# Advancing the next head pair's prologue beside the current pair's heads in an RWKV-7 layer

## Chip, cores, metric

One Trainium2 chip (trn2), all 8 NeuronCores, no exchange between them: each core runs the whole network on its own eight 256-token segments (or one 2048-token sequence). The metric is the device time of the slowest core in microseconds (us).

## The reference, cut to what matters

Four layers; layers 0 and 2 mix tokens with HGRN2, layers 1 and 3 with RWKV-7, each followed by an MLP. Only RWKV-7 is touched. Per direction, head and token:

```python
r, k, v = rkv[0], rkv[1], rkv[2]                    # three projections of the shifted input
decay = exp(-0.606531 * sigmoid(w0 + tanh(xs1 @ w_la) @ w_lb))
a  = sigmoid(a0 + (xs4 @ a_la) @ a_lb)
kk = k * k_k;  kk = kk / max(sqrt(sum(kk * kk, -1)), 1e-12)      # per head
k  = k * (1 + (a - 1) * k_a)
bonus = sum(r * k * r_k, -1) * v
# scan over tokens (forward, and backward on the flipped sequence)
sa = einsum('bzhvk,bzhk->bzhv', s, kk_t)
s  = s * w_t - sa (x) (kk_t * a_t) + v_t (x) k_t
y_t = einsum('bzhvk,bzhk->bzhv', s, r_t)
```

## The kernel before

A core handles 16 tiles of 128 tokens, per layer and direction. Heads are 64 wide, so 128 channels hold a pair; a tile has 8 pairs (`c`). The kernel records operations in program order (`S.op(engine, ...)`) and derives the semaphore waits from the buffers each reads and writes; every engine has its own list, in the order recorded. All instructions carry the recording helper's line, L200, so a reader goes by tile names.

In names of the profile, PE is TensorE's matmul and PEld its weight load, DVE is VectorE, ACT is ScalarE, POOL is GpSimd, `ps` and `PS[n]` are the program's banks of PSUM, which PE's rows write (`ps<-` in every row shown), and a table load (ACT_TABLE_LOAD, 1283 ns each, 1985 of them in the trace before) is the instruction that stands on ACT three times in each prologue: before the sigmoids, before the square root and before the exponentials.

For each pair there is a prologue, then two head generators advanced in turn, one step (up to a `yield`) per round:

```python
for c in range(8):
    pp = PS[0]
    # 8 + 8 projection matmuls (r, k), 2 low-rank matmuls        PE  -> pp
    # sg, aa = sigmoid(...)                                      ACT (table load)
    # kk = pk * k_k                                              DVE
    # kk2 = kk * kk                                              POOL
    # block sum of kk2 (matmul with blockones) -> PS[1]          PE
    # rs = max(.), sqrt(rs)                                      DVE, ACT (table load)
    # rs = 1/rs; kk *= rs; t, k2 (into t)                        DVE
    # bb = kk * aa (into aa)                                     POOL
    # prod = r * r_k * k2 (into kk2); head sum -> PS[7]          DVE, PE
    # Ls = scan(sg); Dsg = difference                            DVE
    # wc, emD, eD, emD2 = exp(...); Ds2                          ACT (table load), POOL
    # KB = (k2*eD, bb*eD), QR = (kk*emD2, r*emD)                 POOL, DVE
    # 3 transposes -> PS[1]; KoT, BoTn                           PE, DVE
    def head_gen(c=c, hh=None, ptb=ptb): ...
    run_interleaved([head_gen(hh=0), head_gen(hh=1)], 2)
```

A head generator has 24 steps: 0 opening matmuls of KB and QR (64 rows high); 1 three masked copies on DVE; 2 and 3 right side RH; 4 to 15 six levels of a triangular solve, each a round of fp32 128x128 matmuls and a round of one DVE addition and up to two ACT copies; 16 and 17 matmuls and copies for the chunk maps; 18 to 21 two state updates (DVE scales, PE multiplies, DVE copies back); 22 output matmuls; 23 copy out. I call 18 to 23 the tail, and a pair's join the time from the last head matmul of one pair to the first of the next.

Of the kernel before, what the change touches and what calls it, by code (L numbers as in the profile page):

```python
# [298 lines left out]
def build_program(n_layers=4, mix=True, dbg=False, stop=None):  # L299
# [46 lines left out]
    with contextlib.ExitStack() as st:  # L346
# [548 lines left out]
        def rwkv_layer(l, j, hT, BhT):  # L895
            with contextlib.ExitStack() as ph:
# [51 lines left out]
                ct["prod"] = ct["kk2"]  # L948
# [5 lines left out]
                ct["wc"] = sb(ph, "c_wc", [128, 2])  # L954
# [6 lines left out]
                Bct["prod"] = Bct["kk2"]  # L961
# [12 lines left out]
                for d in range(2):  # L974
# [14 lines left out]
                    for bi, i in enumerate(order):  # L989
# [40 lines left out]
                        for c in range(8):  # L1030
                            cs = slice(c * 128, (c + 1) * 128)
                            S.skip = (_LIM["rstep"] < 4) or (_rt[0] > _LIM["rtiles"])
                            pp = PS[0]
                            for k in range(8):
                                S.op("pe", lambda e, k=k, cs=cs: e.matmul(out=pp[:, 0:128], lhsT=W3[0][:, k, cs], rhs=xsn[0][:, k, :], start=(k == 0), stop=(k == 7)),
                                     reads=[BW3[0], Bxs[0]], writes=[BPS[0]])
                            for k in range(8):
                                S.op("pe", lambda e, k=k, cs=cs: e.matmul(out=pp[:, 128:256], lhsT=W3[1][:, k, cs], rhs=xsn[2][:, k, :], start=(k == 0), stop=(k == 7)),
                                     reads=[BW3[1], Bxs[2]], writes=[BPS[0]])
                            S.op("pe", lambda e, cs=cs: e.matmul(out=pp[:, 256:384], lhsT=wlb[:, cs], rhs=tw[:], start=True, stop=True), reads=[Blo, Btw], writes=[BPS[0]])  # L1040
                            S.op("pe", lambda e, cs=cs: e.matmul(out=pp[:, 384:512], lhsT=alb[:, cs], rhs=ta[:], start=True, stop=True), reads=[Blo, Bta], writes=[BPS[0]])
                            pr, pk = pp[:, 0:128], pp[:, 128:256]
                            S.skip = (_LIM["rstep"] < 5) or (_rt[0] > _LIM["rtiles"])
                            S.op("act", lambda e, c=c: e.activation(out=ct["sg"][:], in_=pp[:, 256:384], func=AF.Sigmoid, bias=vcol(0)[:, c:c + 1], scale=1.0),
                                 reads=[BPS[0], Bvec], writes=[Bct["sg"]])
                            S.op("act", lambda e, c=c: e.activation(out=ct["aa"][:], in_=pp[:, 384:512], func=AF.Sigmoid, bias=vcol(1)[:, c:c + 1], scale=1.0),
                                 reads=[BPS[0], Bvec], writes=[Bct["aa"]])
                            S.op("dve", lambda e, c=c: e.tensor_scalar(out=ct["kk"][:], in0=pk, scalar1=vcol(2)[:, c:c + 1], scalar2=None, op0=ALU.mult),
                                 reads=[BPS[0], Bvec], writes=[Bct["kk"]])
                            S.op("pool", lambda e: e.tensor_tensor(out=ct["kk2"][:], in0=ct["kk"][:], in1=ct["kk"][:], op=ALU.mult), reads=[Bct["kk"]], writes=[Bct["kk2"]])  # L1050
                            S.op("pe", lambda e: e.matmul(out=PS[1][:, 0:128], lhsT=cF["blockones"][:], rhs=ct["kk2"][:], start=True, stop=True),
                                 reads=[Bk, Bct["kk2"]], writes=[BPS[1]])
                            S.op("dve", lambda e: e.tensor_scalar_max(out=ct["rs"][:], in0=PS[1][:, 0:128], scalar1=1e-24), reads=[BPS[1]], writes=[Bct["rs"]])
                            S.op("act", lambda e: e.activation(out=ct["rs"][:], in_=ct["rs"][:], func=AF.Sqrt), reads=[Bct["rs"]], writes=[Bct["rs"]])
                            S.op("dve", lambda e: e.reciprocal(out=ct["rs"][:], in_=ct["rs"][:]), reads=[Bct["rs"]], writes=[Bct["rs"]])
                            S.op("dve", lambda e: e.tensor_tensor(out=ct["kk"][:], in0=ct["kk"][:], in1=ct["rs"][:], op=ALU.mult), reads=[Bct["kk"], Bct["rs"]], writes=[Bct["kk"]])
                            S.skip = (_LIM["rstep"] < 6) or (_rt[0] > _LIM["rtiles"])
                            S.op("dve", lambda e, c=c: e.tensor_scalar(out=ct["t"][:], in0=ct["aa"][:], scalar1=1.0, scalar2=vcol(3)[:, c:c + 1], op0=ALU.subtract, op1=ALU.mult),
                                 reads=[Bct["aa"], Bvec], writes=[Bct["t"]])
                            S.op("dve", lambda e: e.scalar_tensor_tensor(out=ct["k2"][:], in0=ct["t"][:], scalar=1.0, in1=pk, op0=ALU.add, op1=ALU.mult),  # L1060
                                 reads=[Bct["t"], BPS[0]], writes=[Bct["k2"]])
                            S.op("pool", lambda e: e.tensor_tensor(out=ct["bb"][:], in0=ct["kk"][:], in1=ct["aa"][:], op=ALU.mult), reads=[Bct["kk"], Bct["aa"]], writes=[Bct["bb"]])
                            S.op("dve", lambda e, c=c: e.scalar_tensor_tensor(out=ct["prod"][:], in0=pr, scalar=vcol(4)[:, c:c + 1], in1=ct["k2"][:], op0=ALU.mult, op1=ALU.mult),
                                 reads=[BPS[0], Bvec, Bct["k2"]], writes=[Bct["prod"]])
                            S.op("pe", lambda e, c=c: e.matmul(out=PS[7][:, 2 * c:2 * c + 2], lhsT=ct["prod"][:], rhs=cF["headind"][:], start=True, stop=True),
                                 reads=[Bct["prod"], Bk], writes=[BPS[7]])
                            S.skip = (_LIM["rstep"] < 7) or (_rt[0] > _LIM["rtiles"])
# [10 lines left out]
                            S.op("act", lambda e, Lv=Lv: e.activation(out=ct["wc"][:].unsqueeze(2), in_=Lv[:, :, 63:64], func=AF.Exp, scale=-C0), reads=[Bct["Ls"]], writes=[Bct["wc"]])  # L1078
                            S.op("pool", lambda e: e.tensor_tensor(out=ct["Ds2"][:], in0=ct["Dsg"][:], in1=ct["sg"][:], op=ALU.add), reads=[Bct["Dsg"], Bct["sg"]], writes=[Bct["Ds2"]])
                            S.op("act", lambda e: e.activation(out=ct["emD"][:], in_=ct["Dsg"][:], func=AF.Exp, scale=C0), reads=[Bct["Dsg"]], writes=[Bct["emD"]])  # L1080
                            S.op("act", lambda e: e.activation(out=ct["eD"][:], in_=ct["Dsg"][:], func=AF.Exp, scale=-C0), reads=[Bct["Dsg"]], writes=[Bct["eD"]])
                            S.op("act", lambda e: e.activation(out=ct["emD2"][:], in_=ct["Ds2"][:], func=AF.Exp, scale=C0), reads=[Bct["Ds2"]], writes=[Bct["emD2"]])
                            S.skip = (_LIM["rstep"] < 8) or (_rt[0] > _LIM["rtiles"])
# [4 lines left out]
                            S.skip = (_LIM["rstep"] < 9) or (_rt[0] > _LIM["rtiles"])  # L1088
# [9 lines left out]
                            def head_gen(c=c, hh=None, ptb=ptb):  # L1098
                                head = 2 * c + hh
                                prs = slice(64 * hh, 64 * hh + 64)  # L1100
                                hc = slice(head * 64, head * 64 + 64)
                                hcl = slice(hh * 64, hh * 64 + 64)
                                hx = HX[hh]
                                A1, A2, Nmt, Zmt, RH, RpE, P2T, T0p, wch = hx["A1"], hx["A2"], hx["Nm"], hx["Zm"], hx["RH"], hx["RpE"], hx["P2T"], hx["T0p"], hx["wch"]
                                Bh = hx["B"]
                                PA, PB, BA, BB = PS[2 + 2 * hh], PS[3 + 2 * hh], BPS[2 + 2 * hh], BPS[3 + 2 * hh]
                                qr2 = QR[prs, :, :].rearrange("p a t -> p (a t)")
                                S.op("pe", lambda e: e.matmul(out=PA[:, 0:256], lhsT=KB[prs, 0, :], rhs=qr2, start=True, stop=True), reads=[Bct["KB"], Bct["QR"]], writes=[BA])
                                S.op("pe", lambda e: e.matmul(out=PA[:, 256:512], lhsT=KB[prs, 1, :], rhs=qr2, start=True, stop=True), reads=[Bct["KB"], Bct["QR"]], writes=[BA])
                                S.op("pe", lambda e: e.matmul(out=PB[:, 0:128], lhsT=QR[prs, 0, :], rhs=KB[prs, 1, :], start=True, stop=True), reads=[Bct["KB"], Bct["QR"]], writes=[BB])  # L1110
                                yield
                                S.op("dve", lambda e: e.tensor_tensor(out=A1[:], in0=PA[:, 0:256], in1=mk1[:], op=ALU.mult), reads=[BA, Bdirc], writes=[Bh["A1"]])
# [5 lines left out]
                                yield  # L1118
                                S.op("act", lambda e: e.activation(out=RH[:, 64:128], in_=PB[:, 128:192], func=AF.Copy), reads=[BB], writes=[Bh["RH"]])
                                yield  # L1120
                                for lvl in range(6):
                                    if lvl == 0:
                                        Zc, BZc = A2[:, 0:128], Bh["A2"]
                                    else:
# [228 lines left out]
```

## Time and profile before

| | before |
|---|---|
| median time, 16 runs | 35,234 us |
| four RWKV passes (2 layers x 2 directions), profiled core, each from its first to its last wide POOL instruction | 23,268 us |
| one tile | 364 us |
| pair: prologue alone / heads, mean of the 448 pairs that another follows in their tile | 16.7 / 24.2 us |
| mean granted clock | 0.65 |

A row of the costliest groups reads: line, engine, operation, output<-input, shape, count | busy us, mean ns of one | idle time of the engine just before, and what ended it. In the timeline: start, duration, engine, operation, and in brackets the idle time before it. A row of the window table has PE, PEld, DVE, ACT and POOL busy us (with counts), granted clock, DMA share, GB/s. A granted clock of 0.50 is half speed: in the trace before, successive matmuls of 512 columns in bf16 start 427 ns apart at 0.50 and 216 ns apart at 1.00 (medians). The lines of this profile stand in the prediction.

### The profile page before, as it was taken

The page shows a single profiled execution, that of the slowest core. Times are in us where ns is not written, and L with a number is a line of the kernel's source. Part 1 is how long each engine was busy: PE and PEld are TensorE (multiplying, and loading weights), DVE is VectorE, ACT ScalarE, POOL GpSimd, SP SyncE. Part 2 cuts the span into 40 slices and gives each one's busy share as a digit, 9 for nine tenths or more (in the row PEclk, how much of TensorE's full clock was granted, in tenths as well). Part 3 has the DMA queues.
Part 4 walks back from the last instruction along what each step waited for, and adds up shares of the span by engine and source line. Part 5 has one row for each costly group of instructions (what it writes and reads, how often), then busy time and mean ns, then how long its engine had stood idle before and what let it go on. Part 6 is the DMA issues. An engine that isn't in the chain of part 4 may idle for free.

```text
span 35174.1 us, 407253 instructions; the slowest of 8 cores (35099.4 to 35174.1 us)
## 1 busy us (share of the span) xinstructions
PE 19515.1 (55%) x114368; PEld 15106.0 (43%) x114368; DVE 12249.9 (35%) x34848; ACT 8818.3 (25%) x24259; POOL 4908.3 (14%) x6307
## 2 busy tenths in 40 slices
PE   4333755666556566564643337566665565666646
PEld 3221445555545555553232214455554455555522
DVE  3553223333333333332245532333333333333322
ACT  1222122222222222221122221222222222222211
POOL 1223001111111101111112230110111111011121
PEclk7556766666666666666755567666666666666658
DMA  2001400000000000000310014000000000000004
GB/s 62 18 11 31 73 16 3 2 3 2 3 12 2 3 2 2 3 2 21 54 43 18 11 37 71 12 2 2 3 2 3 12 2 3 2 3 2 2 23 61
DMA packets 563961, 564.35 MB, mean 16 GB/s; under 512 B 71360, under 2 KB 471616, under 8 KB 561792
## 3 DMA queue, kind: packets, MB, share of 16 engines
q0 software_dynamic: 328240, 235.26, 4.9%
q1 hardware_dynamic: 100816, 181.36, 1.5%
q10 hardware_dynamic: 132736, 121.66, 1.2%
q8 instruction: 1012, 16.58, 0.2%
q14 instruction: 1157, 9.48, 0.1%
HBM read 672.80 MB, written 100.66 MB: 22 GB/s over the span
## 4 chain that ended last, share of the span: by engine, by line
PE 46%; DVE 19%; issue 12%; ACT 10%; POOL 7%; DMA 4%; DVEq 1%; another core or an unknown queue 1%; ACTq 0%; POOLq 0%; SPq 0%
PE ps L200 46%; ACT L200 5%; DVE c_kk_u L200 3%; DMA ups_u<-ffn_w_up 2%; DVE h_Tp_u L200 2%; DVE Tst_u L200 2%; POOL yblk_u L200 1%; DVE A_u L200 1%; DVE xs_s_u L200 1%; DVEq L196 1%; POOL lnv_u L200 1%; POOL KB_u L200 1%; DVE c_t_u L200 1%; DVE T0p_u L200 1%; POOL QR_u L200 1%
## 5 line engine op out<-in xcount | busy, mean ns | idle before, releaser
L200 ACT ACT_TABLE_LOAD x1985 | 2546.8, 1283 | 5413.1 <-PE ps L200 1917.6
L200 DVE TENSOR_TENSOR RH_u<-RH_u,ps 128x128 f32<-128x128 f32 x6144 | 1765.5, 287 | 3928.8 <-PE ps L200 3914.8
L200 PE MATMUL ps<-RH_u,Zm_u 128*128 128x128 f32 x10240 | 2399.6, 320 | 195.2 <-ACT Zm_u L200 134.0
L200 POOL TENSOR_TENSOR c_kk_u<-c_kk_u 128x128 f32<-128x128 f32 x512 | 203.9, 398 | 14234.7 <-DVE c_kk_u L200 14234.7
L200 PEld LDWEIGHTS ps<-RH_u,Zm_u 128*128 128x128 f32 x10240 | 1757.6, 215 | 502.2 <-issue 351.5
L200 ACT ACTIVATE Zm_u<-ps 128x128 f32<-128x128 f32 x5120 | 1420.5, 277 | 1847.5 <-PE ps L200 1775.1
L200 PE MATMUL ps<-Zm_u,Nm_u 128*128 128x128 f32 x8192 | 1824.3, 308 | 1.2
L200 PE MATMUL ps<-rc_headind_u,c_kk_u 128*128 128x2 f32 x1024 | 285.1, 348 | 2469.8 <-DVE c_kk_u L200 2469.8
L200 PE MATMUL ps<-QR_u,KB_u 64*128 64x256 f32 x4096 | 1583.9, 671 | 0.0
L200 DVE TENSOR_SCALAR c_kk_u<-ps,rvec_u 128x128 f32<-128x128 f32 x512 | 179.4, 350 | 3553.0 <-ACT c_aa_u L200 3553.0
L200 PEld LDWEIGHTS ps<-Zm_u,Nm_u 128*128 128x128 f32 x8192 | 1404.9, 214 | 4.5 <-issue 4.5
L200 PE MATMUL ps<-ident_u,KB_u 128*128 128x128 f32 x1024 | 338.1, 434 | 1909.2 <-POOL KB_u L200 1909.2
L200 PE MATMUL ps<-rw_u,xs_s_u 128*128 128x512 bf16 x1024 | 369.4, 540 | 1831.4 <-DVE xs_s_u L200 1831.4
L200 PEld LDWEIGHTS ps<-rc_headind_u,c_kk_u 128*128 128x128 f32 x1024 | 255.9, 310 | 2600.9 <-issue 2600.9
L200 PE MATMUL ps<-h_u,ups_u 128*128 128x512 bf16 x4096 | 1044.1, 417 | 573.8 <-DMA ups_u<-ffn_w_up 517.6
L200 PE MATMUL ps<-vf_u,A_u 128*128 128x64 f32 x4096 | 1209.4, 392 | 212.0 <-DVE RH_u L200 207.6
L200 PE MATMUL ps<-c_kk_u,rc_blockones_u 128*128 128x128 f32 x1024 | 378.1, 471 | 1694.4 <-POOL c_kk_u L200 1694.4
L200 PE MATMUL ps<-Nm_u,Zm_u 128*128 128x128 f32 x6144 | 1308.7, 298 | 0.0
L200 ACT ACTIVATE Nm_u<-ps 128x128 f32<-128x128 f32 x4096 | 1137.2, 278 | 384.0 <-ACT Zm_u L200 11.1
L200 PE MATMUL ps<-RH_u,A_u 128*128 128x128 f32 (+1 forms) x4096 | 1207.3, 392 | 0.3
L200 ACT ACTIVATE RH_u<-ps 128x64 f32<-128x64 f32 x1024 | 229.5, 224 | 3885.4 <-DVE RH_u L200 3625.0
L200 PE MATMUL ps<-h_qpp_u,h_kout_u 128*128 128x128 bf16 x512 | 135.7, 265 | 1820.4 <-POOL h_qpp_u L200 1760.0
(231 smaller groups left out, 45101.8 us busy)
## 6 DMA issues: line engine op xcount, KB each, us to landing
ups_u<-ffn_w_up POOLq DMA_DIRECT2D x256, 512.0 KB, 5.9
adas_u<-ada_w ACTq DMA_DIRECT2D x48, 1024.0 KB, 5.3
adas_u<-ada_w SPq DMA_DIRECT2D x48, 1024.0 KB, 5.4
oscr<-oblk_u SPq DMA_DIRECT2D x64, 512.0 KB, 2.6
ot_u<-oscr SPq DMA_DIRECT2D x64, 512.0 KB, 3.3
ot_u<-oscr ACTq DMA_DIRECT2D x64, 512.0 KB, 3.3
wd_u<-ffn_w_down POOLq DMA_DIRECT2D x16, 2048.0 KB, 36.8
oscr<-yblk_u SPq DMA_DIRECT2D x64, 512.0 KB, 2.6
```

Source lines behind the costliest of these rows:

```text
L196: engobj.wait_ge(sem, val)
L200: ins = getattr(engobj, fn[0])(*fn[1], **fn[2])
```

## The change

Intent: run the long chain of the prologue of pair c+1 while PE works on the heads of pair c. The arithmetic is the same; what changes is order, one buffer for `prod` and a second for `wc`, and the PSUM bank of the low-rank products.

```diff
-                ct["prod"] = ct["kk2"]
+                ct["prod"] = sb(ph, "c_prod", [128, 128])
-                ct["wc"] = sb(ph, "c_wc", [128, 2])
+                wcs = [sb(ph, "c_wc%d" % i_, [128, 2]) for i_ in range(2)]
...
-                        for c in range(8):
+                        def proA(c):                 # one step per round
+                            yield; yield             # rounds 0, 1
                             ... r projection, 8 matmuls -> PS[0][:, 0:128]
+                            yield                    # 3
                             ... k projection -> PS[0][:, 128:256]
+                            yield ...                # 9: kk   10: kk2, scan, Dsg
+                            ...                      # 11: block sum  12: max  13: sqrt
+                            ...                      # 16: t  17: k2  18: wc, Ds2, emD
+                            ...                      # 19: prod, eD  20: head sum, emD2
+                            ...                      # 22: reciprocal  23: kk, bb
+                        def proB(c):                 # KB, QR, transposes, KoT, BoTn
+                        def proL(c):                 # 2 low-rank matmuls, now -> PS[6]
+                        def proS(c):                 # 2 sigmoids
...
-                            run_interleaved([head_gen(hh=0), head_gen(hh=1)], 2)
+                        proL(0); proS(0)
+                        for _ in proA(0): pass
+                        proL(1); proB(0); proS(1)
+                        for c in range(8):
+                            gens = [head_gen(c, 0), head_gen(c, 1)] + ([proA(c + 1)] if c < 7 else [])
+                            run_interleaved(gens, 3)
+                            if c < 7:
+                                if c < 6: proL(c + 2)
+                                proB(c + 1)
+                                if c < 6: proS(c + 2)
```

## The prediction

> **What bounds the kernel now.** I read the page's header and slices first, then the chain of work that ended last, then the timeline and the window table around one pair of heads in the RWKV stage, which is the only stage the change touches.
>
> ```profile
> span 35174.1 us, 407253 instructions; the slowest of 8 cores (35099.4 to 35174.1 us)
> PE 19515.1 (55%) x114368; PEld 15106.0 (43%) x114368; DVE 12249.9 (35%) x34848; ACT 8818.3 (25%) x24259; POOL 4908.3 (14%) x6307
> PEclk7556766666666666666755567666666666666658
> PE 46%; DVE 19%; issue 12%; ACT 10%; POOL 7%; DMA 4%; DVEq 1%; another core or an unknown queue 1%; ACTq 0%; POOLq 0%; SPq 0%
> L200 POOL TENSOR_TENSOR c_kk_u<-c_kk_u 128x128 f32<-128x128 f32 x512 | 203.9, 398 | 14234.7 <-DVE c_kk_u L200 14234.7
> ```
>
> No engine is full, all eight cores agree, and the chain changes engine all the time: this is latency, not throughput. The last row's count, 512, is the number of head pairs: 2 RWKV layers x 2 directions x 16 tiles x 8 pairs. The first wide POOL instruction of each tile recurs every 364 us, so the stage takes 64 x 364 = 23.3 ms of the 35.2. The start of each pair's projection recurs every 40.7 us on average (20.8 ms in all). A typical pair in the timeline (start, duration):
>
> ```profile
> 13059.56 1.04 PE L200 MATMUL ps<-xs_r_u,rw_u 128*128 128x128 bf16 x8
> ...
> 13061.86 1.28 ACT L200 ACT_TABLE_LOAD   x1 [1.85 <-PE ps L200]
> ...
> 13066.55 1.28 ACT L200 ACT_TABLE_LOAD   x1 [2.52 <-DVE c_kk_u L200]
> ...
> 13068.26 0.95 DVE L200 RECIPROCAL c_kk_u<-c_kk_u 128x128 f32<-128x128 f32 x1 [1.78 <-ACT c_kk_u L200]
> ...
> 13071.07 1.28 ACT L200 ACT_TABLE_LOAD   x1 [2.91 <-DVE c_Ls_u L200]
> ...
> 13074.89 0.45 POOL L200 TENSOR_TENSOR QR_u<-c_kk_u,c_Ls_u 128x128 f32<-128x128 f32 x1
> 13075.08 0.66 PE L200 MATMUL ps<-ident_u,KB_u 128*128 128x128 f32 x2 [3.72 <-POOL KB_u L200]
> ...
> 13076.26 2.24 PE L200 MATMUL ps<-QR_u,KB_u 64*128 64x256 f32 x6
> ```
>
> From 13059.56 to 13076.26 the pair's prologue runs alone, 16.7 us in which one engine waits for the next. Then the two heads run, interleaved, until the next prologue at 13099.57: 23.3 us here; over seven pairs of four tiles the prologue took 16.7 to 17.0 and the heads 23.3 to 26.1, about 24.0 on average. The windows of that pair (PE busy first, then PEld, DVE, ACT, POOL; granted clock third from the end):
>
> ```profile
> 13059.56:13076.26 16.70, 4.57 (x26) 3.22 (x25) 3.64 (x10) 6.03 (x11) 2.62 (x6) 0.50 0.00 0
> 13076.26:13084.44 8.18, 7.78 (x32) 7.03 (x32) 3.78 (x12) 1.20 (x5) 0.00 (x0) 0.50 0.00 0
> 13084.44:13098.10 13.66, 12.23 (x102) 10.67 (x102) 5.81 (x22) 4.75 (x19) 0.00 (x0) 1.00 0.01 2
> ```
>
> In the prologue PE works 4.57 of 16.7 us; in the heads PE is nearly full, at half clock for the first 8.2 us, and is what sets their length until the low-density tail.
>
> [...] only 0.50 and 1.00 occur away from the switches; in six successive pairs the rise to full came exactly 40.96 us apart[...] and the fall 13.66 or 10.24 us later[...]. [...] the trace has 1283, 1985 times, three in each prologue. [...]
>
> **The change part by part.** No arithmetic is added. The prologue is cut in three. The part up to `kk` and `bb` (proA) becomes a third generator, advanced one step per round beside the two heads of the pair before; its steps are spaced with empty rounds. Between pairs stay the two small low-rank matmuls (proL), the forming and transposing of KB and QR (proB), and the sigmoids (proS), which now run a pair ahead. `prod` gets its own buffer, `wc` two. Pair 0 of a tile keeps an exposed prologue, so 7 of 8, 448 pairs, gain.
>
> Counting yields, head and proA both have about 24 rounds, so each step can be placed.
>
> 1. Rounds 2-3, 16 projection matmuls on PE: at half clock 8 cost 0.85 us (second group starts 0.83 after the first), so 1.7, less some 0.2 of PE wait filled there: +1.5. But they [...] should bring the rise of the clock forward[...] (on average 9.9 us after the heads' start). A level takes 2.6 us at half and 1.57 at full clock. I credit 1.0: net +0.5.
> 2. Round 11 and 20, two fp32 matmul pairs (block sum, head sum), about 0.25 each on PE at full clock: +0.5.
> 3. DVE: `kk`, scan and difference in rounds 9-10 (1.05 us) fit in the levels, where DVE works 0.6 of 1.57 us. `k2` (0.29) and `prod` (0.35) in rounds 17 and 19 stand before the state update: +0.65.
> 4. ACT: the square root's load in round 13 lies where ACT has no further copy for about 1.7 us (13050.16 to 13051.84), needing 1.6; the exponentials' load in round 18 lies in a 4.9 us ACT gap; the sigmoid's load overlaps the first rounds of the next heads, whose first copy comes 4.6 us in. +0.
> 5. What remains exposed between pairs: the last state copy starts at 13056.41; then reciprocal 0.95, product 0.29, POOL `bb` and three products (about 2.0 with gaps), `QR` on DVE 0.3, transpose and handover 0.5: heads can start near 13061.0, against the heads' end at 13059.56. +1.45.
>
> New period: 24.0 + 0.5 + 0.5 + 0.65 + 1.45 = 27.1 us against 40.7-40.75. Saved 13.65 x 448 = 6.12 ms. In pair 0 the scan now stands before the normalisation, so the exponentials no longer wait behind the 3 us of reciprocal and products: 2.5 x 64 = 0.16 ms. Sum 6.28 ms: 35,226 - 6,280, about **28,950 us**.
>
> **Rivals.** (a) *The clock stays full.* Closing a 16.7 us hole might keep PE warm through the joins. That would save about 4 us more per pair (the 8.2 us at half clock shrink by about 3, the tail by 1): period 23, 27.2 ms. For it: the idle hole is what the cold start follows. Against it: the clock falls near 13098.1, before the heads end and while PE shows busy[...]. (b) [...] If the projections cost their full 1.5, one table load stalls a copy (+1.3), and DVE steps slip: period 29.6-30, about 30.2 ms. For it: ACT and PE both lie near their limits in the levels (four copies fill 1.48 of 1.57 us). Against: the empty rounds place the loads where ACT is free. (c) *Single buffers serialise it*: KB, QR, `aa` and `sg` exist once. But KB's last reader is the pair's transpose and its opening matmuls, QR's is round 16, and the sigmoids stand behind `bb`'s use, all done in time. If it did hold, the join would be 4-5 us: 30.3 ms.
>
> **Range and chances.** The net gain per pair is known to some 1.8 us either way, mostly from the clock: 448 x 1.8 = 0.8 ms. Range 28,150 to 29,750 us. A result within 2% would need 12 of the 13.7 us to reappear, which no rival does: faster 0.98, same 0.01, slower 0.01.
>
> **What would show it.** In the changed profile: the pair period near 27 us; first head matmul 1 to 2 us after the last of the pair before; still three table loads per pair; PE's waits for POOL's KB and `kk` products (1909 and 1694 us in the costliest groups before) mostly gone; PE busy share up towards 70%, its busy time down if the clock rises earlier. The granted clock in the RWKV slices tells (a) from my reading: near 0.75 for mine, above 0.9 for (a). I am wrong if the join exceeds 3 us, if a table load sits between two level copies, or if the heads themselves take over 28 us.

It reads 24.0 + 0.5 + 0.5 + 0.65 + 1.45 = 27.1 us per pair, 6.12 + 0.16 = 6.28 ms saved, 28,950 us. The 1.0 us credited in step 1 was the author's estimate, about what one level gains from the full clock (2.6 - 1.57); that the projections bring the rise of the clock forward was not shown before the result (e2 has it: 9.1 us after the heads' start with them there, 10.1 without). The 1283 is the ns of one table load in the profile before.

## The result

| | before | after |
|---|---|---|
| median | 35,234 us (16 runs) | 29,289 us (8 runs) |
| ratio | | 0.8317 (0.8305 to 0.8328) |
| four RWKV passes, profiled core | 23,268 us | 17,228 us |
| everything else, profiled core | 11,906 us | 12,025 us |
| one tile (median) | 364 us | 269.5 us |
| mean granted clock | 0.65 | 0.69 |

A ratio is the mean time of one kernel's runs over the mean of the other's runs of the same rounds, so it is not quite the ratio of the medians. Executions in which one die ran at a lower clock are left out of the means.

The page after, header, engines, clock by slices, chain, and the row that answers to the one shown before:

```profile
span 29252.7 us, 402073 instructions; the slowest of 8 cores (29140.2 to 29252.7 us)
PE 18996.9 (65%) x114368; PEld 14870.7 (51%) x114368; DVE 11985.8 (41%) x34848; ACT 8841.1 (30%) x24259; POOL 4893.1 (17%) x6307
PEclk8556686777776777775856566767777767777758
PE 55%; DVE 18%; issue 10%; DMA 5%; POOL 5%; ACT 5%; DVEq 1%; another core or an unknown queue 1%; ACTq 0%; POOLq 0%; SPq 0%
L200 POOL TENSOR_TENSOR c_kk_u<-c_kk_u 128x128 f32<-128x128 f32 x512 | 204.9, 400 | 7146.6 <-DVE c_kk_u L200 7103.1
```

The counts of the five engines are exactly those of before: nothing was removed. ACT's share of the chain that ended last fell from 10% to 5% and POOL's from 7% to 5%, PE's rose from 46% to 55%. The clock digits of the RWKV slices went from mostly 6 to mostly 7. PE's waits for POOL's KB and `kk` products, 1909 and 1694 us before, are 229 and 74 us now.

The timeline of one join after, without the weight loads:

```profile
10641.13 0.22 DVE L200 COPY rT_u<-ps 64x64 f32<-64x64 f32 x1 [0.41 <-PE ps L200]
10641.27 0.93 DVE L200 RECIPROCAL c_kk_u<-c_kk_u 128x128 f32<-128x128 f32 x1
...
10643.97 1.11 PE L200 MATMUL ps<-T0p_u,RpE_u 64*128 64x64 f32 x4
10644.16 0.45 POOL L200 TENSOR_TENSOR QR_u<-c_kk_u,c_Ls_u 128x128 f32<-128x128 f32 x1
10644.72 0.29 DVE L200 TENSOR_TENSOR QR_u<-ps,c_emD_u 128x128 f32<-128x128 f32 x1 [2.12 <-POOL QR_u L200]
10644.88 0.31 PE L200 MATMUL ps<-tw_u,wlb_u 64*128 64x128 bf16 x1
...
10645.71 0.42 PE L200 MATMUL ps<-ident_u,QR_u 128*128 128x128 f32 x1
```

The heads' last matmul ends at 10645.08 and the next pair's first starts at 10646.06. By 10645.01 DVE and POOL are done with QR, so what is left between the pairs is PE's own work: two low-rank matmuls and three transposes at half clock. The windows of the pair that starts there (start to rise of the clock, full clock, fall to the heads' end, join):

```profile
10646.06:10655.08 9.02, 8.62 (x44) 7.87 (x44) 3.69 (x12) 2.44 (x7) 0.00 (x0) 0.50 0.01 3
10655.08:10668.72 13.64, 11.74 (x100) 10.26 (x100) 7.41 (x30) 8.57 (x26) 0.85 (x2) 1.00 0.00 1
10668.72:10672.70 3.98, 3.98 (x19) 3.58 (x18) 1.53 (x4) 0.22 (x1) 1.73 (x4) 0.50 0.00 0
10672.70:10673.68 0.98, 0.98 (x6) 0.50 (x4) 0.00 (x0) 0.80 (x2) 0.00 (x0) 0.50 0.00 0
```

The pair takes 27.62 us: heads 26.64, join 0.98. PE is now busy 25.3 of them, and yet it runs at half clock for 14 of 27.6 us. The cold stretch at the start (9.02 us) is as long as it was with a 16.7 us hole before it (8.18 in the pair shown before; over all 448 pairs 9.1 against 9.3 on average). After the rise the clock stays full for 13.65 us in every one of the 448 pairs; before, it did so in 322 of them, and for 10.24 us in the other 126.

### The profile page after: what moved, and what is told of

Read it like the earlier page. It is cut to its first block, busy times and chain, and to the rows that moved or that the text cites. A ratio compares the mean times of both kernels' runs of the same rounds, so it can differ in the third digit from the quotient of the medians.

```text
span 29252.7 us, 402073 instructions; the slowest of 8 cores (29140.2 to 29252.7 us)
## 1 busy us (share of the span) xinstructions
PE 18996.9 (65%) x114368; PEld 14870.7 (51%) x114368; DVE 11985.8 (41%) x34848; ACT 8841.1 (30%) x24259; POOL 4893.1 (17%) x6307
## 4 chain that ended last, share of the span: by engine, by line
PE 55%; DVE 18%; issue 10%; DMA 5%; POOL 5%; ACT 5%; DVEq 1%; another core or an unknown queue 1%; ACTq 0%; POOLq 0%; SPq 0%
PE ps L200 55%; DMA ups_u<-ffn_w_up 3%; DVE h_Tp_u L200 2%; DVE Tst_u L200 2%; POOL yblk_u L200 2%; DVE A_u L200 2%; ACT L200 2%; DVE xs_s_u L200 2%; POOL lnv_u L200 1%; DVEq L196 1%; DVE RpE_u L200 1%; DVE T0p_u L200 1%; POOL ot_u L200 1%; DVE h_koe_u L200 1%; DVE Nm_u L200 1%
## 5 line engine op out<-in xcount | busy, mean ns | idle before, releaser
L200 ACT ACT_TABLE_LOAD x1985 | 2546.8, 1283 | 2041.8 <-PE ps L200 1110.7
L200 PE MATMUL ps<-RH_u,Zm_u 128*128 128x128 f32 x10240 | 2274.1, 305 | 140.5 <-ACT Zm_u L200 112.8
L200 PEld LDWEIGHTS ps<-RH_u,Zm_u 128*128 128x128 f32 x10240 | 1616.6, 199 | 477.6 <-issue 253.3
L200 PE MATMUL ps<-vf_u,A_u 128*128 128x64 f32 x4096 | 1311.7, 421 | 210.7 <-DVE RH_u L200 207.0
L200 PEld LDWEIGHTS ps<-Zm_u,Nm_u 128*128 128x128 f32 x8192 | 1285.2, 197 | 5.2 <-issue 5.2
L200 PEld LDWEIGHTS ps<-vf_u,A_u 128*128 128x128 f32 x4096 | 985.5, 298 | 470.0 <-issue 407.8
L200 PE MATMUL ps<-T0p_u,P2T_u 64*64 64x64 f32 x4096 | 662.4, 244 | 823.6 <-DVE T0p_u L200 823.6
L200 PE MATMUL ps<-h_Tp_u,h_qe_u 128*128 128x128 bf16 x2048 | 299.4, 300 | 1336.7 <-DVE h_Tp_u L200 1336.7
L200 PEld LDWEIGHTS ps<-rw_u,xs_s_u 128*128 128x128 bf16 x1024 | 125.6, 127 | 2036.9 <-issue 2004.1
L200 PEld LDWEIGHTS ps<-QR_u,KB_u 64*128 64x128 f32 x4096 | 1023.6, 321 | 245.2 <-issue 150.0
L200 DVE TENSOR_TENSOR A_u<-ps,mk_u 128x256 f32<-128x256 f32 x2048 | 864.5, 422 | 645.8 <-PE ps L200 536.1
```

What stands on the lines that cost most here:

```text
L200: ins = getattr(engobj, fn[0])(*fn[1], **fn[2])
```

## The experiments

Eleven kernels ran, on four chips, each beside the kernel before; all gave correct outputs. My theory after the result (a theory, which the runs below test in part): the gain is the latency chain laid beside PE work; what it costs is PE time of the projections at half clock and DVE time in the tail, and how long PE's clock stays full depends on the matmul work added (e6, e7), not on the hole. "Round n" is the n-th step of the interleaving. A difference between two variants, where I turn it into time, is the difference of their ratios times 35,200 us, and per pair that over 448. Averages "over all pairs" are of the profiled core, over the 448 pairs that another one follows in their tile.

### Is it the overlap? Run the same order without it

```diff
-    gens = [head_gen(c, 0), head_gen(c, 1)] + ([proA(c + 1)] if c < 7 else [])
-    run_interleaved(gens, 3)
+    run_interleaved([head_gen(c, 0), head_gen(c, 1)], 2)
+    if c < 7:
+        for _ in proA(c + 1): pass
```

> The changed kernel's order of work, but the next pair's long part (proA) runs after the two heads have ended instead of beside them. Overlap theory with reordering: the sigmoids run a pair ahead and the scan stands before the normalisation, as in pair 0 of the changed kernel, whose join from first projection to first head matmul was 11.1 us; so period 24.0 + 11.1 = 35.1 us, 7.5 us above the changed kernel's 27.6, total about 29.3 + 3.3 = 32.6 ms. Rival (all of the gain is overlap, the reordering is worth nothing): period near 40, total about 34.8 ms. Rival (the reordering alone gives most of it): under 31 ms.

Measured (e1): 32,818 us, ratio 0.9321. Heads and join of one pair, window table:

```profile
10593.63:10617.03 23.40, 21.60 (x138) 19.05 (x138) 9.59 (x34) 6.00 (x23) 0.00 (x0) 0.79 0.01 2
10617.03:10628.14 11.11, 4.51 (x26) 3.16 (x26) 3.63 (x10) 6.03 (x11) 2.59 (x6) 0.50 0.00 0
```

The join is 11.11 us as expected, against 16.7 before and 0.98 in the changed kernel. So the gain has two parts, and both rivals fall: 2.4 ms (1 - 0.9321) comes from the new order alone, 3.5 ms (0.9321 - 0.8317) from the overlap. The split holds with the new order counted first: overlap without the new order was not run, and it might have hidden much of those 2.4 ms by itself. The prediction counted the whole as overlap; its total did not need the split.

### Do the projections cost their PE time?

```diff
-    round 2: r projection      round 3: k projection
+    round 8: k projection      round 10: r projection
```

> The 8+8 projection matmuls move from rounds 2-3 into rounds 8 and 10, inside the levels, where the clock is mostly full. Theory (projections cost their PE time at the clock in force, 1.7 us at half, 1.1 at full): period 27.6 - 0.6 = 27.0, total about 29.0 ms. Rival (they brought the rise of the clock forward, so moving them gives that back): the rise comes later after the heads' start and the total is the same or up to 0.4 ms longer.

Measured (e2): 28,991 us, ratio 0.8235, 0.29 ms (0.65 us per pair) less than the change. This is the size that the theory names: two groups of matmuls moved into full-clock time cost 1.1 instead of 1.7 us (a group takes 0.85 us at half clock in the trace before, and 0.55 at full clock from its first start to the next matmul's in e9; on the profiled cores the mean period fell by less, from 27.63 to 27.23 us). The rival has a true part: over all pairs the rise of the clock came 10.1 us after the heads' start, against 9.1 in the changed kernel and 9.3 before, and the clock stayed full for 10.24 instead of 13.65 us in 91 of 448 pairs. So in front of the levels the projections do bring the rise 1.0 us forward relative to where it falls without them, but the levels then start 1.7 us later, and the sum is a loss.

### Do the DVE steps in the tail cost their time?

```diff
-    round 16: t     round 17: k2    round 19: prod
+    round 4: t      round 6: k2     round 7: prod
```

> t, k2 and prod move from rounds 16, 17 and 19 to rounds 4, 6 and 7. Theory (k2 and prod stand in DVE's queue before the state update and cost their 0.65 us): period 27.0, total about 29.0 ms. Rival (in the tail they lie in waits, in the levels they delay the RH additions): same or longer than 29.3 ms.

Measured (e3): 28,961 us, ratio 0.8232, 0.30 ms or 0.67 us per pair less than the change; the prediction's step gave 0.65. In the tail PE waits for DVE: its waits for the state scales (`T0p`) fell from 824 to 622 us in the whole run, where the kernel before had 620. In the levels the three steps delayed nothing that shows.

### Does it matter where a table load stands?

```diff
-    rounds 9, 10, 11, 12, 13: kk; kk2, scan, Dsg; block sum; max; sqrt
+    rounds 7,  8,  9, 10, 11: the same
```

> kk to the square root move two rounds earlier, so that the square root and its table load (1.6 us) fall in round 11, between the level copies on ACT, instead of round 13. Theory (ACT is nearly full in the levels, 1.48 of 1.57 us, so a load there stalls them): period +1.3 to +1.6, total 29.9 to 30.0 ms. Rival (PE has work queued that hides it): within 0.2 ms of 29.3.

Measured (e4): 30,083 us, ratio 0.8547: 0.81 ms, 1.8 us per pair, more than the change. ACT's timeline, first in this run, then in the changed kernel:

```profile
10369.26 0.28 ACT L200 ACTIVATE Nm_u<-ps 128x128 f32<-128x128 f32 x1
10369.56 1.28 ACT L200 ACT_TABLE_LOAD   x1
10370.85 0.31 ACT L200 ACTIVATE c_kk_u<-c_kk_u 128x128 f32<-128x128 f32 x1
10371.07 0.43 ACT L200 ACTIVATE Zm_u<-ps 128x128 f32<-128x128 f32 x2
```

```profile
10661.57 0.28 ACT L200 ACTIVATE Zm_u<-ps 128x128 f32<-128x128 f32 x1 [0.40 <-PE ps L200]
10661.87 1.28 ACT L200 ACT_TABLE_LOAD   x1
10663.16 0.31 ACT L200 ACTIVATE c_kk_u<-c_kk_u 128x128 f32<-128x128 f32 x1
10663.57 0.17 ACT L200 ACTIVATE wch_u<-ps 64x2 f32<-64x2 f32 x1
```

In the first the load stands before the level's copies (`Zm`), which PE needs for the last level; in the second the last `Zm` is out and the next copy for the heads (`wch`) is not due before 10663.57. Where the load stands is worth 1.8 us a pair. The time was slightly above the range I had named. Over all pairs the full-clock time of a pair was 13.6 us, as in the changed kernel, and the time at half clock rose by 2.0 us, which fits a stall that pushes later work past the fall of the clock; this was not tested.

### Put the projections where PE waits

The projections run two pairs ahead, even pairs into `PS[0]`, odd ones into free columns of `PS[7]`, as a fourth generator:

```diff
+    def ppof(c):
+        return (PS[0][:, 0:256], BPS[0]) if c % 2 == 0 else (PS[7][:, 128:384], BPS[7])
-    round 2: r(c + 1)          round 3: k(c + 1)
+    round 17: k(c + 2)         round 19: r(c + 2)
```

> The projections run one more pair ahead, into a second PSUM place, in rounds 17 and 19 of the tail, where PE waits for DVE. Theory: PE's wait there (0.6 and 0.3 us) swallows most of their 1.1 us at full clock, so the heads lose 1.5 us: period about 26.1, total about 28.6 ms. If the dense work also keeps the clock from falling in the tail, period about 23, total about 27.3 ms. Rival (they only move and still cost their time): 29.0 to 29.3 ms.

Measured (e5): 28,521 us, ratio 0.8094, 0.78 ms less than the change (1.75 us per pair). Two windows, heads and join:

```profile
10399.06:10423.69 24.63, 23.56 (x159) 20.95 (x158) 12.36 (x43) 10.19 (x32) 1.95 (x5) 0.78 0.01 1
10423.69:10425.24 1.55, 1.24 (x5) 0.47 (x3) 0.29 (x1) 1.39 (x2) 0.63 (x2) 0.50 0.00 0
```

The heads lose 2.2 us over all pairs, and the join grows from 1.0 to 1.7: from the last state copy to the heads' end it is 2.86 us here and was 3.95 in the join shown above, so the chain of reciprocal, product and POOL work is no longer covered, which is the kind of exposure that the prediction's fifth step had put at 1.45. After a rise the clock stays full for 13.7 us in most pairs and for 17.1 in a third of them, where the changed kernel had 13.7 in all; it still falls about once per pair, and 400 of 448 pairs start at half clock.

### Why does the clock fall? Add matmuls of no use

A fourth generator adds 5 bf16 matmuls with 256 columns in each of the rounds 17, 19 and 21; they write free columns of `PS[6]` that nobody reads.

```diff
+    def proD():
+        # rounds 17, 19, 21:
+        for k in range(5):
+            matmul(out=PS[6][:, 256:512], lhsT=W3[0][:, k, 0:128], rhs=W3[1][:, k, 0:256])
```

> The changed kernel plus 15 matmuls of no use (bf16, 256 columns[...]) in rounds 17, 19 and 21 of every pair; the outputs do not depend on them. It asks why the clock falls. Theory[...]: the clock stays full through more of the tail and the next heads' start, the mean granted clock rises from 0.69 to over 0.8 and the total is the same or shorter in spite of the added work (28.0 to 29.3 ms). Rival (the fall is a fixed time after the rise, 10.24 or 13.66 us, whatever PE does): clock as before and the total longer by the part not in PE's waits, 0.5 to 0.9 us per pair, 29.5 to 29.7 ms.

Measured (e6): 28,908 us, ratio 0.8213. Half clock, full clock and half clock again, windows cut where the clock changes:

```profile
10289.48:10299.72 10.24, 9.84 (x51) 9.17 (x50) 3.93 (x13) 2.26 (x8) 0.00 (x0) 0.50 0.00 0
10299.72:10316.79 17.07, 15.88 (x129) 13.39 (x128) 8.86 (x32) 9.92 (x27) 2.59 (x6) 1.00 0.01 2
10316.79:10323.61 6.82, 6.42 (x37) 5.76 (x36) 3.08 (x11) 1.00 (x4) 0.00 (x0) 0.50 0.01 2
```

The kernel does 15 useless matmuls more per pair and is 0.37 ms faster than the changed one. The clock stays full for 17.1 us in most pairs instead of 13.7, so the fall is not a fixed time after the rise; the rival is out. The mean clock of the cores was 0.72 to 0.73, below the 0.8 I had named: the fall comes 3.41 us later (17.07 against 13.66) but still comes. On the profiled core 21 full-clock stretches lasted 24 to 89 us; two pairs in one of 65 us took 23.7 and 23.9 us.

### What a full clock is worth

The same with 8 more in round 1, 4 in round 22 and 8 in the join, 35 per pair in all.

```diff
+    dummies: {1: 8, 17: 5, 19: 5, 21: 5, 22: 4}, and 8 between proL and proB
```

> As the run with useless matmuls in rounds 17, 19 and 21, with more of them at the places where the clock still fell there: 8 in round 1, 4 in round 22, 8 in the join. It asks what the first rival of the prediction is worth, a clock that stays full. Theory ([...] a full clock shortens pairs to the 23.7 us seen in two pairs of that run): mean granted clock in the RWKV stage above 0.9, period 23.5 to 24.5, total 27.4 to 27.9 ms. Rival (the pairs at full clock were a stray of one core[...]): clock near 0.8 and the added work costs, total 28.9 to 29.4 ms.

Measured (e7): 27,924 us, ratio 0.7929, just outside the range I had named. One pair, heads and join, then a thousand us of the stage:

```profile
10208.07:10230.74 22.67, 21.53 (x181) 18.63 (x181) 12.37 (x43) 11.60 (x33) 1.98 (x5) 1.00 0.00 1
10230.74:10232.70 1.96, 1.96 (x17) 1.38 (x16) 0.29 (x1) 0.40 (x2) 0.60 (x2) 1.00 0.00 0
...
10000.00:11000.00 1000.00, 812.94 (x6476) 678.79 (x6476) 480.55 (x1494) 408.18 (x1134) 159.98 (x229) 0.90 0.01 4
```

```profile
10000.00:11000.00 1000.00, 779.56 (x4812) 668.64 (x4813) 435.80 (x1342) 367.52 (x1022) 151.71 (x210) 0.70 0.01 4
```

The first fence is this run, the second the changed kernel over the same stretch. Clock 0.90 against 0.70; in 46 of the 64 tiles one full-clock stretch of 188 or 191 us covers nearly all the pairs, and the clock falls only between tiles. A pair takes 24.4 us (median) with 35 matmuls too many. So the first rival of the prediction would have been worth the 1.4 ms that this run gains, or more without its useless work, had the change made it come true; it did not: in the changed kernel the hole was gone, and the clock fell all the same until matmul work was added.

### Better versions

All use the projections two pairs ahead (rounds 17 and 19), `t`, `k2` and `prod` in rounds 4, 6 and 7, and the reciprocal in round 20 with its products in 21; two add useless matmuls.

```diff
-    round 22: reciprocal   round 23: kk, bb
+    round 20: reciprocal   round 21: kk, bb
     with the edits of rounds 4/6/7 and 17/19 above
+    e8:  dummies {1: 8, 21: 5, 22: 4}, 8 in the join
+    e10: dummies {1: 8}
+    e11: dummies {1: 8, 21: 5}
```

> The same without the useless matmuls. Theory: 28.5 (projections in the tail) less 0.3 (DVE steps out of the tail) less 0.4 (reciprocal off the join): 27.8 ms, clock near 0.72. Rival (with the DVE waits gone, other waits take their place): 28.2 to 28.5 ms.

Measured (e9): 27,647 us, ratio 0.7844, no useless work. The pair shown now has heads of 22.68 and a join of 0.98:

```profile
10098.83:10121.51 22.68, 20.87 (x159) 18.53 (x158) 12.37 (x44) 11.39 (x33) 2.58 (x6) 0.91 0.01 2
10121.51:10122.49 0.98, 0.98 (x7) 0.50 (x4) 0.09 (x1) 0.81 (x2) 0.00 (x0) 0.50 0.00 0
```

The parts add, and a little more: against the projections in the tail alone (0.8094), 0.88 ms, of which 0.30 is what the DVE steps gave by themselves. The other 0.58 was not split: the reciprocal left the join (0.9 us over all pairs against 1.7), and the clock stayed full longer (16.4 us of a pair against 14.7).

> Projections in the tail rounds 17 and 19 a pair ahead, t, k2, prod early, the reciprocal in round 20 and its products in 21, and useless matmuls in rounds 1 (8), 21 (5), 22 (4) and the join (8). Theory: the gains add, 0.3 ms from DVE, 0.7 from the projections, 0.4 from the join, and with a full clock throughout 1.0 to 1.5 more: 26.6 to 27.3 ms. Rival (at full clock ACT's copies and DVE set the pace of the levels and nothing more comes): 27.4 to 27.8 ms, as the run with useless matmuls alone.

Measured (e8): 27,605 us, ratio 0.7837, the same as without the useless matmuls. My theory expected 26.6 to 27.3 and missed. The clock did rise (0.78 mean over the cores against 0.72), and over all pairs the heads are 1.3 us shorter (21.9 against 23.2), but the joins are 1.2 us longer (2.1 against 0.9): the matmuls placed in the join stand on the path, and they cost what the clock gave.

> The combined version plus only 8 useless matmuls in round 1, where PE waits for DVE's masked copies. Theory: PE's hole there swallows them and [...] the clock falls less often or rises sooner: clock in the stage from 0.77 to about 0.85, total 27.0 to 27.4 ms against 27.65. Rival (they stand in PE's queue and cost what the clock gives): 27.5 to 27.8 ms.

Measured (e10): 27,537 us, ratio 0.7815. This is the rival's range: the clock of the stage went to 0.80 to 0.81, but little time came of it (0.4%, inside the intervals of the two ratios).

> The combined version plus 8 useless matmuls in round 1 and 5 in round 21, none in the join or round 22. Theory: clock about 0.9, period near 23.0, total 26.9 to 27.3 ms. Rival (the run with these and 12 more in round 22 and the join showed 27.60, no gain, so the filling itself does not pay once the useful work is spread): 27.4 to 27.8 ms.

Measured (e11): 27,067 us, ratio 0.7681, the best of all.

```profile
10129.23:10150.85 21.62, 20.37 (x172) 17.81 (x171) 12.50 (x44) 11.68 (x33) 2.63 (x6) 1.00 0.01 2
10150.85:10151.36 0.51, 0.51 (x5) 0.31 (x3) 0.02 (x1) 0.35 (x2) 0.00 (x0) 1.00 0.00 0
```

With 13 useless matmuls in two places where PE waits anyway, and none in the join, pairs take 22.0 us (median) at full clock (0.85 to 0.89 over the stage). Against e8, which differs by the 12 matmuls of round 22 and the join alone, it shows that in this version those 12 cost 0.55 ms. The place written to matters too: the useless matmuls write the bank that the sigmoids read, and so they waited 331 times for a sigmoid, 103 us in all.

## Why the prediction was right, and where it was off

The time (29,289) lies within the range and 1.2% above the point (28,950). The saving in the RWKV passes was 6.04 ms against 6.28.

- **What bounds it: right.** The serial chain was the cost; over all pairs the period fell from 40.9 to 27.6 us, the instruction counts unchanged.
- **Step 1, the projections: the wrong term.** It charged 1.5 us and credited 1.0 for an earlier rise of the clock. The rise came 9.1 us after the heads' start against 9.3 before (the prediction had read 9.9), so the levels, starting 1.7 us later, are cold for a shorter time by about that much, and the full-clock time of a pair grew from 12.7 to 13.65 us; but it did not pay the 1.0. Over all pairs the heads grew from 24.24 to 26.63 us, by 2.39, where the prediction summed 1.65 (0.5 + 0.5 + 0.65). The missing 0.74 us, 0.33 ms at 448 pairs, is three quarters of the credit; whether another term holds a part of it was not separated. That the projections do cost time where they stood is shown: moving them away gained 0.65 us (e2) and 1.75 us (e5). The sample behind the prediction's 24.0 and 40.7 was 0.2 us low in both, which does not touch the saving.
- **Step 2, two small matmul groups (0.5): not tested apart.** With the projections at their full 1.5 the heads sum to 24.24 + 1.5 + 0.5 + 0.65 = 26.89 against 26.63, which says only that the errors together are small.
- **Step 3, DVE: right.** 0.65 predicted, 0.67 by moving `t`, `k2` and `prod` away.
- **Step 4, table loads cost nothing: right for the square root's**, whose load and root fit between the last `Zm` and `wch` in the lines above, and it was the round that made it so: two rounds earlier costs 1.8 us. This is also where the order of ACT's queue shows in a number: in e4 the copies `Zm` that stand behind the load start 1.51 us after it does (10369.56 to 10371.07). In the changed kernel a load starts 0.02 us after the ACT instruction before it ended (median of 1,984), and the next one starts 1.29 us after the load did (all 1,984). The loads of the exponentials and the sigmoids were not tested.
- **Step 5, the join: 1.45 predicted, 1.0 found over all pairs.** The sum is also wrong: the terms listed add to 4.04 us and end at 13060.45, 0.9 us after the heads, so the sum as listed meets the 1.0 by luck, since another engine set it: in the changed kernel the chain takes about as long as it says (3.88 us from the last state copy to the end of `QR`) and ends just before the heads do, because the matmuls after that copy ran at half clock and took 3.95 us instead of 3.15; PE's own low-rank matmuls and transposes were left. This gave back 0.20 ms. With the tail shortened (e5), the chain stood there with 1.7.
- **Rival (a), clock stays full: rightly rejected.** With the hole gone the clock falls all the same, 13.65 us after each rise, and e6 and e7 show that added matmul work postpones the fall (to 17.1 us after the rise in most pairs of e6) or removes it within a tile (in 46 of the 64 tiles of e7 one stretch of 188 or 191 us). What makes the clock fall was not shown: the size of the tail's matmuls, their number and the waits between them are not separated. The price put on it, period 23, lies near the 23.7 us pairs of e6 and the 24.4 of e7, which carry useless work; no run has a full clock without it. That only 0.50 and 1.00 occur holds for the trace before (24,351 and 10,452 us); the trace of the changed kernel shows a third, 0.81, for 264 us in all, outside the pairs.
- **Rival (b): its pieces exist** (projections at full cost, a load between copies), each measured, but only the first was in the change.
- **Rival (c), single buffers: did not happen**; the join shows no wait on a reader of the pair before. It does show a wait within the pair: DVE's half of QR waits for POOL's half of the same buffer (2.12 us idle), behind PE's work here.
- **The clock figure 0.75 for the RWKV slices was too high:** 0.70 to 0.72, which is the same miss as in step 1.
- **The split was not foreseen:** 40% of the gain (2.4 of 5.9 ms) is reordering when that is counted first, which the prediction credited only to pair 0 of each tile. The total does not suffer, as a hidden chain need not be short. For pair 0 itself it had 2.5 us; the time from a tile's last head matmul to the first of the next fell by 2.3 (52.6 to 50.3).

What stays open: what makes the clock rise and fall. Long idle gaps of PE do not explain the fall: in the changed kernel none in any of the 448 pairs exceeds 1.42 us, and the clock still fell once per pair. Before the rise PE is busy 8.62 of 9.02 us by the profile in the pair shown, in part with the opening matmuls, 64 rows high; no run here separates rows, columns and idle time.

## What to carry to other kernels

When a profile shows a chain hopping between half-idle engines next to a stretch in which one engine is full, advance the chain step by step beside that stretch, and choose each step's slot by what stands behind it in that engine's queue: a 1.3 us table load was hidden in one round, and two rounds earlier it made each pair 1.8 us longer. Count moved matmuls at the clock in force where they land (1.7 us at half, 1.1 at full for the two projections), and try them where PE waits. And look at the granted clock of every stage before calling PE full: here half of each pair ran at half speed with PE busy, and some matmul work in the gaps was worth more than it cost: 15 useless matmuls per pair took 0.37 ms off (0.8317 to 0.8213), 13 in the combined version 0.57 ms (0.7844 to 0.7681), while 25 with 12 of them in the join and round 22 gave nothing (0.7844 to 0.7837).
